# The order of sixteen products in a feed-forward block, and the place of one cast in the last gate

## The chip, the cores and the metric

The kernel runs on one core of a Trainium2 chip. The core has a matrix engine (TensorE, PE in the profile, with its weight loads listed apart as PEld), VectorE (DVE), ScalarE (ACT), GpSimd (POOL), and SyncE (SP), which issues most of the DMAs; GpSimd issues the rest. Each engine works its own instructions in the order in which they were written into its queue and waits on semaphores for the others. The metric is the device time of one execution in microseconds; the time before is the median of three runs.

## The reference

One layer of a streaming encoder on 512 frames of width 1024, all in float32:

```
h = h + 0.5 * swiglu(rmsnorm(h) , ffn1)          # 1024 -> 2 x 2816 -> 1024
z = rmsnorm(h) @ w_in                            # conv, attention and gate inputs
h = h + concat([conv_module(z), gated_linear_attention(z)]) @ w_out
h = h + 0.5 * swiglu(rmsnorm(h), ffn2)
gate = sigmoid(rmsnorm(h) @ ple_w_gate)          # 1024 x 1024
h = h + gate * (p @ ple_w_proj)                  # 256 -> 1024
out = rmsnorm(h)
```

where `swiglu(x) = (silu(gate) * up) @ w_out` and `gate, up` are the two halves of `x @ w_in`. The change touches the two `swiglu` blocks and the line with `gate`.

## The kernel before

**Numbers in two parts.** Every float32 operand of a product is split into a high part (a cast to fp32r on ScalarE, `high`, L216) and a low part (the operand minus its high part, on VectorE, `low`, L226; `parts`, L238, is both). A product is then three: high by high, high by low, low by high. Some low parts are made another way: ScalarE writes the negative and a DMA of GpSimd adds the operand onto it (`added`, L231). Weights lie in rings of six tiles, `wh` and `wl`.

**The feed-forward blocks** (`ffn`, L663) take two blocks of 128 columns of the hidden width at a time, a pair, and form the pair's gate and up values for all 512 frames by seven quarter products in place of eight (sums and differences of the weights' quarters, `Left`, L436, and of the activations' quarters, `Right`, L372). A quarter is 512 x 256 of weights by 512 x 256 of activations, so it has four blocks of rows (k) and two of columns (i). Five of the seven (`mul`, L341) are 24 products of 256 columns each. The other two, m7 (L744) and m4 (L752), go to both halves of the output, and are written as `mul2` (L357): the high weights times the activations' high and low parts side by side, one *wide* product of 512 columns, and the low weights times the high part, one *narrow* product of 256 columns. Both add into `pd`, a tile of two banks, one for each i. Ahead of m7 stands m6, which is narrow; ahead of m4 stands, in all pairs but one, a piece of the second product (`second`, L825), whose 512-column products read `act`. Of the first network nine pairs run this way, of the second ten. The order of TensorE, VectorE and ScalarE is here that of the program's text.

**The gate** (from L1770) is one more product by quarters, and in it the scheduler decides the order, bound only by what is needed and by the dependencies that the text adds: `act.behind(x, y)` puts x behind y on ScalarE (class `Ordered`, L36). Its names: `x_` and `w_` are two pairs of banks in which the quarters add up; `t1`, `t2`, `t3` are sums and differences of the weights' quarters. `t2` is made as a difference on VectorE, used, and then a DMA of GpSimd adds the last quarter of the weights onto it (L1803); the result, the second difference, has its parts in `b4` (L1821). `later_high` (L1773) is `high` with the cast put behind the instruction that `squared` names, the last of ScalarE when it was set, which is ahead of the gate.

`inputs(t, e)` (L1667) makes for a block of 128 frames and a half of the width the product with `p` (`pq`) and the transposed `h` (`pt`). `body` (L1714) takes the sum of the gate's product, forms the sigmoid on ScalarE, the product with `pq` and the sum with `pt` on VectorE (`cv`), then on ScalarE the squares of `cv` with their sum (the tile `u`), and multiplies `cv` by the final norm's gain `gfin` on VectorE. `kept` (L1761) copies a bank on ScalarE, `plus` (L1766) adds another bank to the copy on VectorE (tile `sq`).

The banks come from a ring of five with two spare (`bank`, L123). In the gate `x_` and `w_` hold four of the five, so `pq` and `pt` of `inputs(2, 1)`, which both come from the fifth, share it in turn: the transposes into `pt` can start when VectorE has read `pq`.

Of the kernel before, what the change touches and what calls it, by code (L numbers as in the profile page):

```python
# [15 lines left out]
P = 128  # L16
# [15 lines left out]
HALF = SEQ // 2  # L32
# [30 lines left out]
def block_kernel(ctx: ExitStack, tc: tile.TileContext, a: dict, out: bass.AP):  # L63
    nc = tc.nc
    pe, dve, act, pool = (Ordered(tc, e) for e in (nc.tensor, nc.vector, nc.scalar, nc.gpsimd))
# [38 lines left out]
    def tmp(s, w=SEQ, dt=F32, bufs=2):  # L104
        return tp.tile([P, w], dt, tag=s, bufs=bufs, name=nm(s))
# [17 lines left out]
    def bank():  # L123
        turn_no[0] += 1
        if not narrow_only[0] and turn_no[0] % 7 in (5, 6):
            return spare()
        return pp.tile([P, SEQ], F32, tag="mm", bufs=5, name=nm("ps"))
# [88 lines left out]
    def high(r3):  # L216

        nk, nc_ = r3.shape[1], r3.shape[2]
        hi = wp.tile([P, 1024], F32R, tag="wh", bufs=6, name=nm("wh"))
        lo = wp.tile([P, 1024], F32R, tag="wl", bufs=6, name=nm("wl"))  # L220
        h3 = hi[:, :nk * nc_].rearrange("p (k c) -> p k c", k=nk)
        l3 = lo[:, :nk * nc_].rearrange("p (k c) -> p k c", k=nk)
        act.copy(h3, r3)
        return h3, l3, r3

    def low(w, engine=dve):  # L226
        h3, l3, r3 = w
        engine.tensor_tensor(out=l3, in0=r3, in1=h3.bitcast(F32), op=ALU.subtract)
        return h3, l3
# [8 lines left out]
    def parts(r3):  # L238

        return low(high(r3))  # L240
# [20 lines left out]
    def rows_of(w, k):  # L261

        part, kk = (w[k // 4], k % 4) if isinstance(w, list) else (w, k)
        return part[0][:, kk, :], part[1][:, kk, :]
# [89 lines left out]
    def two(t):  # L354
        return t.rearrange("p (k c) -> p k c", k=2)

    def mul2(ps, w, x, first, last):  # L357

        wh, wl = w
        for k in range(4):  # L360
            both_, xh = x[k]
            for i in range(2):
                cs = slice(i * P, (i + 1) * P)
                pe.matmul(two(ps[:, i]), wh[:, k, cs], both_, start=(first and k == 0), stop=False, skip_group_check=True)
                pe.matmul(ps[:, i, 0:HALF], wl[:, k, cs], xh, start=False, stop=last and k == 3, skip_group_check=True)

    def sub(out, x, y):
        dve.tensor_tensor(out=out, in0=x, in1=y, op=ALU.subtract)
# [685 lines left out]
    ps = bank()  # L1054
    for k0 in range(0, DC, 4):
        for i in range(2):
            for j in range(4):
                pe.matmul(ps[2 * RANK * j:2 * RANK * (j + 1)], gw[:, k0 + j, :], hg[k0 + j][i].bitcast(F32),
                          start=(k0 == i == 0), stop=(k0 + i == 5), skip_group_check=True)
# [13 lines left out]
    for j in range(2):  # L1073
        ps = bank()
# [91 lines left out]
    def tokblock(w, t, mid={}):  # L1166

        ps = bank()
        ts = slice(t * P, (t + 1) * P)
        i = 0  # L1170
        for k in range(DC):
            wh, wl = w[k // 2][:2]
            xh, xl = hg[k]
            for x, y in ((xh, wh), (xl, wh), (xh, wl)):
                if i in mid:
                    mid[i]()
                pe.matmul(ps, x[:, ts], y[:, k % 2, :], start=(i == 0), stop=(i == 3 * DC - 1))
                i += 1
        return ps
# [31 lines left out]
    def chunk_sums(cs):  # L1211
        for j in range(2):
            if len(kvs) == j:
                kvs.append([bank(), bank()])
            for c in cs:
                s0 = (c % 2) * CH
                for i in range(2):
                    h = 2 * j + i
                    pe.matmul(kvs[j][c % 2][i * HK:(i + 1) * HK, (c // 2) * HV:(c // 2 + 1) * HV],
                              kdt[j][s0:s0 + CH, (c // 2) * P + i * HK:(c // 2) * P + (i + 1) * HK],  # L1220
                              vt[c // 2][s0:s0 + CH, h * HV:(h + 1) * HV], start=True, stop=True)
# [22 lines left out]
    def outputs(t2):  # L1244
        ops.extend([bank(), bank()])
        for t in (2 * t2, 2 * t2 + 1):
            for h in range(4):
                pe.matmul(out_of(t, h), sc[h][:, t, :], vt[t][:, h * HV:(h + 1) * HV],
                          start=(t % 2 == 0 and h < 2), stop=False, skip_group_check=True)
        for t in (2 * t2, 2 * t2 + 1):  # L1250
            for j in range(2):
                for i in range(2):
                    c = 2 * t + i
                    for h in (2 * j, 2 * j + 1) if c else ():
                        d = slice((h % 2) * HK, (h % 2 + 1) * HK)
                        pe.matmul(out_of(t, h)[i * CH:(i + 1) * CH], qdec[j][d, c * CH:(c + 1) * CH],
                                  states[j][c][0][d], start=False, stop=(t % 2 == j == 1), skip_group_check=True)
        for t in (2 * t2, 2 * t2 + 1):
            junk = tmp("sq", bufs=3)
            for h in range(4):  # L1260
                act.activation(junk[:, h * HV:(h + 1) * HV], out_of(t, h), AF.Square,
                               accum_out=so[:, 4 * t + h:4 * t + h + 1])
# [7 lines left out]
    for t in range(TB):  # L1270
        ps = tokblock(wv, t, {5: lambda: chunk_sums(range(6)),
                             8: lambda: wr.append(high(raw_r[2])),
                             14: lambda: wr.append(high(raw_r[3]))} if t == 3 else {})
# [57 lines left out]
    for t in range(TB):  # L1331
        if t == 0:
            taps(3)
            ps = tokblock(wr, t, {5: lambda: chunk_sums([6]), 12: lambda: outputs(0)})
            chain(range(4, 7))
            oload(4)
        elif t == 1:
            ps = tokblock(wr, t, {2: lambda: outputs(1)})
# [8 lines left out]
        else:  # L1347
            ps = tokblock(wr, t)
# [117 lines left out]
    for k in range(4):  # L1466
        for n in range(3):
            w, ps = half[n]
            wh, wl = rows_of(w, k)
# [70 lines left out]
    q11, q21, q12, q22, b11, b21, t2, wproj = ([] for _ in range(8))  # L1540
# [108 lines left out]
    def times(ps, x, w, first=False, last=False, blocks=((0, 1),), cols=slice(0, SEQ)):  # L1649

        for group in blocks:
            for k in range(4):
                xh, xl = x[k]
                wh, wl = (t[:, k % 2, cols] for t in w[k // 2][:2])
                for i in group:
                    ts = slice(i * P, (i + 1) * P)
                    o = ps[i][:, cols]
                    begin, end = first and k == 0, last and k == 3
                    pe.matmul(o, xh[:, ts], wh, start=begin, stop=False, skip_group_check=True)
                    pe.matmul(o, xl[:, ts], wh, start=False, stop=False, skip_group_check=True)  # L1660
                    pe.matmul(o, xh[:, ts], wl, start=False, stop=end, skip_group_check=True)
# [19 lines left out]
    def parts_of(t, e, z, pq, pt, c0=0, c1=SEQ, by=act):  # L1681

        cs = slice(c0, c1)
        first = t not in hf
        if first:
            hn = hf[t] = cvt()
        elif c0 == 0:
            hn = hl[t] = tmp("g1")
        else:
            hn = hl[t]  # L1690
        sg, junk = tmp("s"), tmp("u1")
        act.activation(sg[:, cs], z[:, cs], AF.Sigmoid, scale=rs[:, t:t + 1])
        yield
        dve.tensor_tensor(out=sg[:, cs], in0=sg[:, cs], in1=pq[:, cs], op=ALU.mult)
        yield
        dve.tensor_tensor(out=hn[:, cs], in0=pt[:, cs], in1=sg[:, cs], op=ALU.add)
        yield
        ss = ssf[:, 2 * t + 1 - first:2 * t + 2 - first] if c1 == SEQ else sse[:, 8:9]
        if by is dve:
            dve.scalar_tensor_tensor(out=junk[:, cs], in0=hn[:, cs], scalar=1.0, in1=hn[:, cs],  # L1700
                                     op0=ALU.mult, op1=ALU.mult, accum_out=ss)
        else:
            act.activation(junk[:, cs], hn[:, cs], AF.Square, accum_out=ss)

        base = sse[:, t:t + 1]
        if first:
            dve.tensor_tensor(out=hn, in0=hn, in1=gfin[e], op=ALU.mult)
            dve.tensor_scalar(base, ss, 1.0 / D, EPS, ALU.mult, ALU.add)
        elif c1 < SEQ:
            dve.scalar_tensor_tensor(out=base, in0=ss, scalar=1.0 / D, in1=base, op0=ALU.mult, op1=ALU.add)  # L1710

        yield

    def body(*args):  # L1714
        for _ in parts_of(*args):
            pass
# [44 lines left out]
    def kept(ps, name, **kw):  # L1761
        o = tmp(name, **kw)
        act.copy(o, ps)
        return o
# [6 lines left out]
    squared, summed = act.latest, dve.latest  # L1771

    def later_high(t):  # L1773

        w = high(t)
        act.behind(act.latest, squared)
        return w
# [27 lines left out]
    pool.on = False  # L1805
    body(0, 0, z0, *i0)
    body(1, 0, z1, *i1)
    b1 = [parts(t1[0])]
    both = tmp("m", 2 * SEQ, bufs=1).rearrange("p (f c) -> p f c", f=2)
    for i in range(2):  # L1810
# [7 lines left out]
    row_last(1)  # L1818
    project(1)
    times(x_, s1_, b1)  # L1820
    b4 = [parts(t) for t in t2]  # L1821
    x5 = [kept(p_, "sq", bufs=3) for p_ in x_]
    i2 = inputs(2, 1)
    z2 = plus(w_[0], x5[0])
# [66 lines left out]
```

## Time and profile before

| | us |
|---|---|
| runs shown | 944.18, 945.10, 945.73 |
| median | 945.1 |
| the profiled execution: its own time | 944.54 |
| its span, first to last instruction | 942.8 |
| TensorE busy | 929.8 (99%) |
| VectorE busy | 785.5 (83%) |
| ScalarE busy | 483.5 (51%) |
| the chain that ended last: TensorE's share | 96% |

A row of the page's groups reads: line, engine, operation, output and inputs by the program's names, shapes, count, then busy time and the mean of one in ns, then the engine's idle time ahead of it and who ended it. All operations are recorded by one helper, so each has the line L46, and tiles tell the places apart: `pd` is written by m7 and m4 alone, `t` is an operand of m7 and `hg` of m4. A row of the timeline reads: start and length in us, engine, line, operation, output and inputs, shapes, count, and in brackets the idle time ahead of it with its cause. Products on TensorE overlap, so the distance between two starts tells what one costs, not its length.

### The profile page before, as it was taken

Reading aid. Unit: us, or ns where it says so; the run is one execution under the profiler, and the core shown is the slowest. Engines: PE = TensorE matmul, PEld = TensorE weight load, DVE = VectorE, ACT = ScalarE, POOL = GpSimd, SP = SyncE. Lnnn points to the kernel's source line nnn. Section 1 sums busy time; section 2 is a strip of 40 time slices with the busy share of each in tenths; the row PEclk is TensorE's granted clock in tenths of the full one; section 3 lists DMA queues with packets and bytes.
Section 4 is the critical chain, followed back from the end, with each engine's and each line's share of the span. In section 5 each row is a group of like instructions: output and inputs, shape, how many; then the busy total and the mean of one; then the engine's idle time right before and its main releaser. Section 6 shows DMA issues by size and latency. Waiting matters only on the chain.

```text
span 942.8 us, 14171 instructions
## 1 busy us (share of the span) xinstructions
PE 929.8 (99%) x5611; PEld 816.0 (87%) x5611; DVE 785.5 (83%) x1077; ACT 483.5 (51%) x730; POOL 55.8 (6%) x74
## 2 busy tenths in 40 slices
PE   8999999999999999999999999999999999999996
PEld 7898999899989888788877889999899999988875
DVE  6798997898789676999986779988888878876986
ACT  5874444344444474463565875454334433446873
POOL 0100000000000111001120020000000000001120
PEclk9999999999999999999999999999999999999999
DMA  7633332342223593256552563432243224347463
GB/s 228 185 105 118 112 101 90 104 134 92 87 91 112 147 261 85 67 127 142 135 134 83 141 158 89 135 107 72 91 135 112 73 88 132 116 153 201 90 111 112
DMA packets 108134, 114.45 MB, mean 121 GB/s; under 512 B 5203, under 2 KB 96517, under 8 KB 108068
## 3 DMA queue, kind: packets, MB, share of 16 engines
q1 hardware_dynamic: 101748, 94.67, 32.7%
q0 software_dynamic: 6304, 18.88, 11.1%
q8 instruction: 44, 0.72, 0.3%
q14 instruction: 22, 0.18, 0.1%
q10 hardware_dynamic: 16, 0.00, 0.0%
HBM read 93.61 MB, written 2.10 MB: 102 GB/s over the span
## 4 chain that ended last, share of the span: by engine, by line
PE 96%; DMA 1%; DVE 1%; ACT 0%; SPq 0%; issue 0%; POOLq 0%; DVEq 0%; ACTq 0%
PE ps L46 84%; PE pd L46 11%; PE ax L46 1%; DMA sm<-in_ple_w_gate 1%; DMA wr<-in_ffn_w_in 1%; ACT wh L46 0%; SPq L538 0%; DVE s L46 0%; SPq L500 0%; DVE u L46 0%; DVE rs L46 0%; ACT yc L46 0%; DVE y L46 0%; DVE cv L46 0%; DVE g L46 0%
## 5 line engine op out<-in xcount | busy, mean ns | idle before, releaser
L46 PE MATMUL ps<-hg,wh 128*128 128x256 f32 (+1 forms) x1232 | 262.4, 312 | 1.2 <-ACT hg L46 1.2
L46 DVE TENSOR_TENSOR wl<-wr,wh 128x1024 fp32r<-128x1024 f32 (+2 forms) x161 | 188.1, 1179 | 38.2 <-ACT wh L46 38.1
L46 PEld LDWEIGHTS ps<-hg,wh 128*128 128x128 f32 x1232 | 201.3, 190 | 16.0 <-ACT hg L46 1.9
L46 ACT CAST wh<-wr 128x1024 fp32r<-128x1024 f32 (+2 forms) x178 | 177.7, 1020 | 49.3 <-DMA wr<-in_ffn_w_out 25.5
L46 PE MATMUL ps<-hg,wl 128*128 128x256 f32 (+1 forms) x616 | 187.6, 311 | 0.0
L46 PE MATMUL ps<-act,wh 128*128 128x512 f32 x512 | 157.9, 390 | 0.0
L46 ACT ACTIVATE s<-g 128x512 f32<-128x512 f32 x48 | 30.4, 632 | 192.2 <-DVE g L46 192.2
L46 PEld LDWEIGHTS ps<-hg,wl 128*128 128x128 f32 x616 | 117.0, 190 | 6.4
L46 PEld LDWEIGHTS ps<-act,wh 128*128 128x128 f32 x512 | 95.0, 188 | 19.0
L46 PE MATMUL ps<-t,wh 128*128 128x256 f32 x608 | 110.9, 283 | 0.0
L46 PE MATMUL ps<-act,wl 128*128 128x512 f32 x256 | 99.6, 389 | 0.0
L46 PEld LDWEIGHTS ps<-t,wh 128*128 128x128 f32 x608 | 95.7, 191 | 2.2
L46 PE MATMUL ps<-t,wl 128*128 128x256 f32 x304 | 86.0, 283 | 0.0
L46 DVE SCALAR_TENSOR_TENSOR cv<-glu,cw,cv 128x502 f32<-128x502 f32 (+24 forms) x90 | 61.8, 729 | 0.3
L46 DVE TENSOR_TENSOR wl<-sm,wh 128x1024 fp32r<-128x1024 f32 x42 | 51.2, 1221 | 8.8 <-ACT wh L46 8.8
L46 PEld LDWEIGHTS ps<-t,wl 128*128 128x128 f32 x304 | 58.2, 192 | 0.0
L46 PEld LDWEIGHTS ps<-act,wl 128*128 128x128 f32 x256 | 48.1, 188 | 10.1
L46 PE MATMUL ps<-wh,hg 128*128 128x512 f32 x176 | 54.7, 392 | 0.0
L46 PE MATMUL pd<-t,wh 128*128 128x512 f32 x152 | 54.6, 399 | 0.0
L46 PE MATMUL pd<-hg,wh 128*128 128x512 f32 x152 | 54.3, 397 | 0.0
L46 DVE SCALAR_TENSOR_TENSOR h<-ps,h 128x512 f32<-128x512 f32 x80 | 51.7, 683 | 2.5 <-PE ps L46 2.4
L46 ACT COPY sq<-ps 128x512 f32<-128x512 f32 x42 | 24.5, 586 | 56.9 <-PE ps L46 56.9
(307 smaller groups left out, 1568.4 us busy)
## 6 DMA issues: line engine op xcount, KB each, us to landing
wr<-in_ffn_w_in SPq DMA_DIRECT2D x84, 512.0 KB
wr<-in_ffn_w_out SPq DMA_DIRECT2D x32, 512.0 KB
wr<-in_w_in SPq DMA_DIRECT2D x20, 512.0 KB
wl<-wr POOLq DMA_DIRECT2D x18, 512.0 KB, 5.2
wr<-in_ffn_w_out SPq DMA_DIRECT2D x16, 384.0 KB
wr<-in_w_out SPq DMA_DIRECT2D x8, 512.0 KB
wq<-in_ple_w_gate SPq DMA_DIRECT2D x8, 512.0 KB
wl<-wq POOLq DMA_DIRECT2D x8, 512.0 KB, 4.9
```

The costliest lines, as they stand in the source:

```text
L46: inst = call(*args, **kwargs)
```

## The change

```diff
     def mul2(ps, w, x, first, last):
 
         wh, wl = w
-        for k in range(4):
-            both_, xh = x[k]
-            for i in range(2):
-                cs = slice(i * P, (i + 1) * P)
-                pe.matmul(two(ps[:, i]), wh[:, k, cs], both_, start=(first and k == 0), stop=False, skip_group_check=True)
-                pe.matmul(ps[:, i, 0:HALF], wl[:, k, cs], xh, start=False, stop=last and k == 3, skip_group_check=True)
+        at = [(k, i, slice(i * P, (i + 1) * P)) for k in range(4) for i in range(2)]
+        for k, i, cs in at:
+            pe.matmul(two(ps[:, i]), wh[:, k, cs], x[k][0], start=(first and k == 0), stop=False, skip_group_check=True)
+        for k, i, cs in at:
+            pe.matmul(ps[:, i, 0:HALF], wl[:, k, cs], x[k][1], start=False, stop=last and k == 3, skip_group_check=True)
...
     body(0, 0, z0, *i0)
     body(1, 0, z1, *i1)
+    squared = act.latest
     b1 = [parts(t1[0])]
...
     times(x_, s1_, b1)
-    b4 = [parts(t) for t in t2]
+    b4 = [low(later_high(t)) for t in t2]
     x5 = [kept(p_, "sq", bufs=3) for p_ in x_]
```

In `mul2` the eight wide products of a quarter product now follow each other, and the eight narrow ones follow them. In the gate the mark `squared` is set anew behind the second block's squares, and the two casts of the second difference go behind it. No instruction is added or taken away.

On TensorE, at the first m7, the order before (a row for each run of like instructions; the last figures are partitions and columns):

```order
L46 MATMUL ps_652<-t_109_565,wl_621 128x256
L46 MATMUL pd_797<-t_114_590,wh_648 128x512
L46 MATMUL pd_797<-t_114_590,wl_649 128x256
L46 MATMUL pd_797<-t_114_590,wh_648 128x512
L46 MATMUL pd_797<-t_114_590,wl_649 128x256
```

and now:

```order
L46 MATMUL ps_652<-t_109_565,wl_621 128x256
L46 MATMUL pd_797<-t_114_590,wh_648 128x512 x4
L46 MATMUL pd_797<-t_115_593,wh_648 128x512 x4
L46 MATMUL pd_797<-t_114_590,wl_649 128x256 x4
L46 MATMUL pd_797<-t_115_593,wl_649 128x256 x4
L46 MATMUL ps_652<-t_124_636,wh_644 128x256 x2
```

Wide and narrow took turns sixteen times in a block; now they change once. All 38 blocks change in this way.

On ScalarE, in the gate (`wh_8759` are the high parts of `p`'s weights, `wh_8789` and `wh_8793` those of the second difference, the `u` rows the squares of the first two blocks):

```order
 L46 CAST wh_8759<-pw_8329 128x512 x2
-L46 CAST wh_8789<-sm_8543 128x1024
 L46 ACTIVATE u_1380_8696,ssf_8513<-cv_8694 128x512
 L46 ACTIVATE u_1383_8705,ssf_8513<-cv_8703 128x512
+L46 CAST wh_8789<-sm_8543 128x1024
```

One cast went from ahead of the two squares to behind them. The scheduler moved one instruction of VectorE as well, at the same place (`wl_8751` is the low part of the first difference's second half, `s_8754` that of an activation):

```order
-L46 TENSOR_TENSOR wl_8751<-wq_8273,wh_8750 128x1024
 L46 TENSOR_TENSOR cv_8694<-cv_8694,gfin_8471 128x512
 L46 TENSOR_SCALAR sse_8514<-ssf_8513 128x1
 L46 TENSOR_TENSOR cv_8703<-cv_8703,gfin_8471 128x512
 L46 TENSOR_SCALAR sse_8514<-ssf_8513 128x1
+L46 TENSOR_TENSOR wl_8751<-wq_8273,wh_8750 128x1024
 L46 TENSOR_TENSOR s_8754<-s_1351_8547,s_8754 128x512
```

`wl_8751` went from ahead of the two multiplications by `gfin` to behind them. Further on, TensorE's order in the gate is the same before and now. There the second row's accumulation (`ps_8720`) and the transposes into `ps_8802`, the `pt` of `inputs(2, 1)`, wait for VectorE, and the rest of the accumulation stands behind the transposes:

```order
L46 MATMUL ps_8719<-wh_8789,hg_8421 128x512 [waits DVE_49]
L46 MATMUL ps_8719<-wh_8789,hg_8421 128x512
L46 MATMUL ps_8719<-wl_8790,hg_8421 128x512
L46 MATMUL ps_8720<-wh_8789,hg_8421 128x512 [waits DVE_49]
L46 MATMUL ps_8720<-wh_8789,hg_8421 128x512
L46 MATMUL ps_8802<-ident,h_100 128x128 [waits DVE_49]
```

The last wait is for VectorE's product that reads `ps_8801`, the `pq` of the same call.

## The prediction

> **What bounds the kernel now.** I read the page's span and its chain of waits first, then the two stages that the change touches: the quarter products in the two feed-forward networks by a table of windows and by TensorE's timeline, and the per-layer gate by the timelines of all engines.
>
> ```profile
> span 942.8 us, 14171 instructions
> PE 96%; DMA 1%; DVE 1%; ACT 0%; SPq 0%; issue 0%; POOLq 0%; DVEq 0%; ACTq 0%
> ...
> 60.00:330.00 270.00, 270.00 (x1741) 246.41 (x1741) 229.37 (x273) 113.53 (x150) 4.86 (x8) 1.00 0.36 107
> 566.00:850.00 284.00, 284.00 (x1858) 260.48 (x1857) 243.24 (x286) 120.05 (x156) 0.00 (x0) 1.00 0.35 108
> ```
>
> TensorE sets the time: it is 96% of the chain, and the two windows, which cover nearly all of both networks, show it busy 270.00 of 270.00 and 284.00 of 284.00 us at a granted clock of 1.00. VectorE is busy 229 of 270 and 243 of 284 us there, so 15% of its time is spare. A nanosecond saved between two products therefore shortens the span, and a wait removed on another engine doesn't.
>
> **The quarter products.** `mul2` runs twice for each pair (m7, m4): 8 wide products (high weights, 512 columns) and 8 narrow ones (low weights, 256 columns). No product, load or cast is added or removed; only the order on TensorE changes.
>
> ```profile
> 65.63 2.83 PE pd L46 x16
> 79.68 2.81 PE pd L46 x16
> ...
> L46 PE MATMUL pd<-t,wh 128*128 128x512 f32 x152 | 54.6, 399 | 0.0
> L46 PE MATMUL pd<-hg,wh 128*128 128x512 f32 x152 | 54.3, 397 | 0.0
> ```
>
> The first two rows are of the chain (start, length, count), the others of the groups by line and shape. 304 wide products are 38 blocks of 8, 19 of m7 and 19 of m4. A block takes 2.83 us where narrow products stand ahead of it (m7) and 2.81 where wide ones do (m4, but for one), alternating. The durations of about 398 ns overlap, so I use the distance from start to start. What the new order costs can be read off where the kernel already runs wide behind wide and narrow behind narrow:
>
> ```profile
> 74.05 0.40 PE L46 MATMUL ps<-actH,wh 128*128 128x512 f32 x1
> 74.29 0.40 PE L46 MATMUL ps<-actL,wh 128*128 128x512 f32 x1
> ...
> 75.44 0.61 PE L46 MATMUL ps<-act,wh 128*128 128x512 f32 x2
> 75.89 0.39 PE L46 MATMUL ps<-act,wl 128*128 128x512 f32 x1
> ...
> 79.52 0.39 PE L46 MATMUL pd<-hg,wh 128*128 128x512 f32 x1
> 79.75 0.28 PE L46 MATMUL pd<-hg,wl 128*128 128x256 f32 x1
> ```
>
> ```profile
> 122.00 0.40 PE L46 MATMUL ps<-t,wh 128*128 128x256 f32 x2
> ...
> 122.95 0.28 PE L46 MATMUL ps<-t,wl 128*128 128x256 f32 x1
> ```
>
> At 74.05 a run of wide products starts behind narrow ones: 8 of them reach to 75.89, 1.84 us, the first at 0.24, later ones at 0.227 (18 from 75.44 to 79.52, 4.08 us). At 122.00 narrow products start behind wide ones: 8 of them reach to 122.95, 0.95 us. So an m7 block becomes 1.84 + 0.95 = 2.79 (was 2.83), an m4 block 8 x 0.227 + 0.95 = 2.77 (was 2.81): about 0.043 us each, 38 x 0.043 = 1.6 us. Put differently, a wide product costs about 0.01 us more behind a narrow one, today eight times in a block, then once. Bounds: if the last wide product, with a narrow one behind it, keeps its dearer step, 0.009 us a block is lost and 1.3 remain; if the dear first steps vanish too, a block is 8 x 0.227 + 8 x 0.119 = 2.77 in both cases and 1.8 is gained. I take 1.6.
>
> A wide product reads its activations in two pieces of 256 columns and changes the bank with each product. The first wide product of the m4 block, at 79.52 behind other wide ones, has both habits and its successor starts 0.23 later, so I charge nothing for them. The second half of the activations is wanted about 0.5 us earlier than now; were it just in time today, one such block would lose up to 0.5, but the two windows show no wait at all, so I charge nothing. The narrow products want the low weights 1.6 us later than today, a slack that no wait asks for.
>
> **The gate.** Here is the one stall of TensorE's tail.
>
> ```profile
> 907.21 0.39 PE L46 MATMUL ps<-wh,s 128*128 128x512 f32 x1
> 909.81 0.50 PE L46 MATMUL ps<-wh,s 128*128 128x512 f32 x1 [2.22 <-DVE s L46]
> 910.15 0.40 PE L46 MATMUL ps<-wl,s 128*128 128x512 f32 x1
> ...
> 916.80 0.60 PE L46 MATMUL ps<-ident,h 128*128 128x128 f32 x4
> ```
>
> ```profile
> 902.52 0.63 ACT L46 CAST wh<-pw 128x512 fp32r<-128x512 f32 x1
> 906.04 1.05 ACT L46 CAST wh<-sm 128x1024 fp32r<-128x1024 f32 x1 [2.89 <-DMA sm<-in_ple_w_gate]
> 906.99 0.62 ACT L46 ACTIVATE u<-cv 128x512 f32<-128x512 f32 x1
> 907.62 0.61 ACT L46 ACTIVATE u<-cv 128x512 f32<-128x512 f32 x1
> 908.57 1.04 ACT L46 CAST wh<-sm 128x1024 fp32r<-128x1024 f32 x1 [0.24 <-DMA sm<-in_ple_w_gate]
> ...
> 911.99 0.59 ACT L46 COPY sq<-ps 128x512 f32<-128x512 f32 x1 [0.38 <-PE ps L46]
> 913.45 0.57 ACT L46 COPY sq<-ps 128x512 f32<-128x512 f32 x1
> 914.89 1.32 ACT L46 ACTIVATE s<-sq,rs 128x512 f32<-128x512 f32 x2
> ```
>
> ```profile
> 902.83 0.68 DVE L46 TENSOR_TENSOR cv<-ax,s 128x512 f32<-128x512 f32 x1
> 903.82 1.22 DVE L46 TENSOR_TENSOR wl<-wq,wh 128x1024 fp32r<-128x1024 f32 x1
> 907.74 0.69 DVE L46 TENSOR_TENSOR cv<-cv,gfin 128x512 f32<-128x512 f32 x1 [2.70 <-ACT u L46]
> 909.08 0.68 DVE L46 TENSOR_TENSOR s<-s,s 128x512 fp32r<-128x512 f32 x1
> ...
> 913.95 1.28 DVE L46 TENSOR_TENSOR sq<-ps,sq 128x512 f32<-128x512 f32 x2
> ...
> 915.74 1.27 DVE L46 TENSOR_TENSOR s<-s,ps 128x512 f32<-128x512 f32 x2
> ...
> 920.34 0.14 DVE L46 TENSOR_SCALAR sse<-ssf 128x1 f32<-128x1 f32 x1
> 921.12 1.37 DVE L46 TENSOR_TENSOR m<-ps,m 128x512 f32<-128x512 f32 x2 [0.64 <-PE ps L46]
> ```
>
> Read upward from 909.81: TensorE waits for a low part (DVE s, 909.08), which stands behind two multiplications by `gfin` (from 907.74), which wait for ScalarE's squares (906.99), which stand behind the cast of the second difference, which waits for its DMA until 906.04. The change puts the squares ahead of that cast. The cast itself loses nothing by it: the squares are done before its DMA lands, and so the casts queued behind it stand where they stood; GpSimd's and SyncE's queues keep their order. In the times of the old trace: the casts of `pw` end at 903.15, VectorE's second `cv` at 903.51, so the squares run to about 904.3; the two multiplications with their small ops (1.34 from 907.74 to 909.08) run 903.8 to 905.2, the moved `wl` (1.22) to 906.4, the low part to 907.0. TensorE wants it at 907.44 (907.21 + 0.23) and `wl` later still, so that stall goes, with 0.4 us to spare.
>
> Now what is late next. TensorE would run on 2.4 us earlier, but ScalarE doesn't: both casts still wait for DMAs that land at about 906.0 and 908.5, and from 908.57 it works without a pause to 911.61, where it waited 0.38 for the product that it copies. That 0.38 is all that it gains: copies at 911.61 and 913.07, sigmoid at 914.51. VectorE's second sum follows the second copy, 913.7 to 914.35. TensorE ran without a pause from 909.81 to the transposes at 916.80, with two products of the second row just ahead of them (from 916.34); from 907.44 it would reach that row at about 913.9 and waits there for 0.5. Behind it stand the four transposes (916.80 in the trace): in the order they wait for VectorE's product that frees the bank, and that follows the sigmoid, 915.36 to 916.04 where it was 915.74 to 916.42. The transposes start at 916.08 in place of 916.80: 0.72 earlier. Less the dearer first product after a wait (909.81 to 910.15 is 0.34 in place of 0.23), 0.6 us remains of a stall of 2.4. Bounds: 0.4, ScalarE's own gain, and 2.4, if the two later waits were no waits. VectorE's small work between (to 920.48 in the trace, 0.38 earlier then) ends at 920.1, before the next sums at 921.12 - 0.6 = 920.5 need it, so the rest of the tail moves with TensorE.
>
> **Sum.** 1.6 + 0.6 = 2.2 us. The profiled execution took 944.5 us (span 942.8, 1.7 around it) and becomes 942.3; it lies 0.6 below the median shown, 945.1. Against that median the forecast is 942.9 us.
>
> **The rivals.** *The blocks don't care about order*, and only the gate gains: 945.1 - 0.6 = 944.5. For it: the same sixteen products stream the same columns. Against it: 0.227 and 0.119 in pure runs add to less than the 0.352 of today's pairs. [...] Chance 0.12.
>
> *The whole stall is won*: the waits at 914.4 and 916.1 don't form because the DMAs land earlier. 945.1 - 1.6 - 2.4 = 941.1. Against it: what issues those DMAs is untouched. Chance 0.08.
>
> *The wide products are slow in this place themselves*, by their two-piece operand or the change of bank, not by their neighbour:
>
> ```profile
> 80.21 0.40 PE L46 MATMUL pd<-hg,wh 128*128 128x512 f32 x1
> ...
> 80.45 0.28 PE L46 MATMUL pd<-hg,wl 128*128 128x256 f32 x1
> ```
>
> Inside a block they do take 0.24. Then a block is 8 x 0.24 + 0.95 = 2.87, 0.05 over today's 2.82: 1.9 us lost, 945.1 + 1.9 - 0.6 = 946.4, slower than before. It turns slower from a wide step of (2.82 + 0.016 - 0.95) / 8 = 0.236 on. Against it: the 0.23 at 79.52. Chance 0.12; a step over 0.242 would carry it past 947.0.
>
> **How the numbers follow.** The forecast has 0.68, its own range 942.6 (1.8 + 0.7, nothing lost at the restart) to 943.4 (1.3 + 0.4). With the indifferent order inside, the range is 941.3 to 944.7, which leaves out the fully won stall and the slow wide products, 0.20. A measurement of this kernel tells about 0.2% from no change, that is 943.2 and 947.0. Faster: 0.61 of the forecast's 0.68 and the 0.08 of the won stall, 0.69. Same: the rest of the forecast, 0.07, the 0.12 of the indifferent order and half of the slow wide products, 0.25. Slower: 0.06.
>
> **What would show it.** In the chain, blocks of 16 at 2.79 and 2.77 us in place of 2.83 and 2.81; wide steps of 0.227 from the fifth on. In the gate, the squares at once behind the casts of `pw`, no wait for the low part near 907, and two new waits on TensorE about 7 us later in sum nearly as long as the old one. Blocks at 2.82 or more, or wide steps of 0.236, would make the first term wrong; a second sum or a sigmoid that comes more than 0.4 us earlier against the DMA's landing, the second.

## The result and the profile after

The changed kernel takes 941.66 us (median of 7 runs, 941.34 to 942.36), the kernel before 944.32 us (median of 7, 944.18 to 945.94): a ratio of 0.9968, 95% interval 0.9956 to 0.9979, so 0.32% faster. The forecast was 942.9 us, in a range of 941.3 to 944.7. It was set against a median of three runs, 945.1, which these seven put at 944.3. The medians lie 2.66 us apart where 2.2 were forecast; the interval of the ratio reaches from 2.0 to 4.2 us, so the times alone don't tell the two apart, and the terms are judged by the traces.

| | before | after |
|---|---|---|
| median, us | 944.32 | 941.66 |
| profiled execution, us | 944.54 | 941.44 |
| its span, us | 942.8 | 939.7 |
| all 38 blocks of quarter products, us | 107.22 | 105.65 |
| TensorE's waits in the gate, us | one of 2.2 | two, 0.3 and 0.8 |

The blocks' sum is the distance from the first product of a block to the first one behind it, added over the 38 blocks of the trace. Of the two waits, 0.8 is the profile's idle time, as 2.2 is; 0.3 is read from the starts (911.58 to 912.10, 0.52 in place of 0.23), of which the profile counts 0.12 as idle.

The chain of waits of the changed kernel (start, length, count), first blocks of the first network and the stretch after the gate's stall:

```profile
PE 97%; DMA 1%; ACT 1%; DVE 1%; issue 0%; POOLq 0%; ACTq 0%; DVEq 0%
...
65.13 2.79 PE pd L46 x16
79.15 2.77 PE pd L46 x16
93.14 2.79 PE pd L46 x16
110.41 2.77 PE pd L46 x16
124.40 2.79 PE pd L46 x16
...
913.66 8.19 PE ps L46 x39
```

TensorE is still the chain. The same blocks read 2.83 and 2.81 before, and the alternation of m7 and m4 is kept. That TensorE still has no pause in the second network is in the table of windows (length, then busy time of TensorE, its weight loads, VectorE, ScalarE, GpSimd, then granted clock):

```profile
566.00:850.00 284.00, 284.00 (x1856) 261.00 (x1855) 243.59 (x286) 119.40 (x156) 0.00 (x0) 1.00 0.35 107
```

Earlier wanted activations and later wanted low weights made no wait. Inside a block, on TensorE's timeline (start, time from the first start to the last modelled end):

```profile
64.97 2.00 PE L46 MATMUL pd<-t,wh 128*128 128x512 f32 x8
66.81 1.12 PE L46 MATMUL pd<-t,wl 128*128 128x256 f32 x8
67.76 0.40 PE L46 MATMUL ps<-t,wh 128*128 128x256 f32 x2
...
78.99 1.98 PE L46 MATMUL pd<-hg,wh 128*128 128x512 f32 x8
80.80 1.11 PE L46 MATMUL pd<-hg,wl 128*128 128x256 f32 x8
81.76 0.40 PE L46 MATMUL ps<-hg,wh 128*128 128x256 f32 x2
```

Starts are what counts: the m7 block's wide part reaches from 64.97 to 66.81, 1.84, its narrow part to 67.76, 0.95; the m4 block's 1.81 and 0.96. These are the two numbers that the forecast had taken from other places of the kernel.

The gate, on TensorE, ScalarE and VectorE (in square brackets the idle time ahead and what ended it):

```profile
911.58 0.39 PE L46 MATMUL ps<-wl,hg 128*128 128x512 f32 x1
912.10 0.73 PE L46 MATMUL ps<-wh,hg 128*128 128x512 f32 x2
913.66 0.66 PE L46 MATMUL ps<-ident,h 128*128 128x128 f32 x4 [0.83 <-DVE s L46]
914.07 0.47 PE L46 MATMUL ps<-wl,hg 128*128 128x512 f32 x1
914.39 0.62 PE L46 MATMUL ps<-wh,hg 128*128 128x512 f32 x2
```

```profile
900.02 1.15 ACT L46 CAST wh<-pw 128x512 fp32r<-128x512 f32 x2
901.06 0.64 ACT L46 ACTIVATE u<-cv 128x512 f32<-128x512 f32 x1
...
901.68 0.62 ACT L46 ACTIVATE u<-cv 128x512 f32<-128x512 f32 x1
...
903.85 1.05 ACT L46 CAST wh<-sm 128x1024 fp32r<-128x1024 f32 x1 [1.45 <-DMA sm<-in_ple_w_gate]
906.37 1.06 ACT L46 CAST wh<-sm 128x1024 fp32r<-128x1024 f32 x1 [1.46 <-DMA sm<-in_ple_w_gate]
...
908.80 0.61 ACT L46 CAST s<-s 128x512 fp32r<-128x512 f32 x1
909.32 0.57 ACT L46 COPY sq<-ps 128x512 f32<-128x512 f32 x1
...
912.18 1.32 ACT L46 ACTIVATE s<-sq,rs 128x512 f32<-128x512 f32 x2
```

```profile
904.30 0.68 DVE L46 TENSOR_TENSOR s<-s,s 128x512 fp32r<-128x512 f32 x1
...
911.35 0.69 DVE L46 TENSOR_TENSOR sq<-ps,sq 128x512 f32<-128x512 f32 x1 [0.74 <-ACT sq L46]
...
912.92 1.30 DVE L46 TENSOR_TENSOR s<-s,ps 128x512 f32<-128x512 f32 x2 [0.28 <-ACT s L46]
```

The squares follow the casts of `pw` at once (901.06), the low part is done at 904.98, and TensorE runs past the place of the old stall. It stops twice later, as forecast: at the second row of the accumulation, which starts at 912.10 behind VectorE's second sum (911.35 + 0.69), and at the transposes (913.66), behind VectorE's product that frees their bank (912.92 and half of 1.30). Both of those wait for ScalarE.

Where the profile's 3.10 us went: 0.50 to the first microseconds, which the change doesn't touch, 1.40 to the two networks, 1.12 to the gate and 0.08 to the rest. The blocks' own sum fell by 1.57, but the networks are only 1.40 shorter. From the first product of a network's first block to the tenth behind its last block, the first network takes 259.54 us before and 258.87 after, the second 279.56 and 278.83. So 0.17 is given back behind the blocks: in each pair of the first network one step among the `act` products is 7 to 8 ns longer than before. The gate's 1.12 is what TensorE gains from the casts of `pw` on (902.00 before, 900.02 after, 1.98) to the end. In the first microseconds the kernel before waited for `hg`, and the changed one in this execution didn't:

```profile
7.82 1.17 PE L46 MATMUL ps<-hg,wh 128*128 128x512 f32 x4
9.89 1.19 PE L46 MATMUL ps<-hg,wh 128*128 128x512 f32 x4 [0.90 <-ACT hg L46]
```

```profile
8.17 2.30 PE L46 MATMUL ps<-hg,wh 128*128 128x512 f32 x8
```

The first rows are of before, the last of after. Of seven experiments whose kernels all start alike, one shows that wait (0.70) and six don't, so it is scatter between executions and no gain. The change's own 1.40 + 1.12 = 2.52 lies near the 2.66 of the medians and inside the interval.

### The profile page after: what moved, and what is told of

Its sections match the earlier page's. It is cut to its first block, busy times and chain, and to the rows that moved or that the text cites. A ratio compares the mean times of both kernels' runs of the same rounds, so it can differ in the third digit from the quotient of the medians.

```text
span 939.7 us, 14172 instructions
## 1 busy us (share of the span) xinstructions
PE 929.2 (99%) x5611; PEld 816.8 (87%) x5611; DVE 785.9 (84%) x1077; ACT 483.1 (51%) x730; POOL 55.9 (6%) x74
## 4 chain that ended last, share of the span: by engine, by line
PE 97%; DMA 1%; ACT 1%; DVE 1%; issue 0%; POOLq 0%; ACTq 0%; DVEq 0%
PE ps L46 84%; PE pd L46 11%; PE ax L46 1%; DMA sm<-in_ple_w_gate 1%; ACT s L46 0%; DVE s L46 0%; ACT wh L46 0%; ACT wl L46 0%; ACT sq L46 0%; DVE u L46 0%; DVE rs L46 0%; ACT yc L46 0%; DVE y L46 0%; DVE g L46 0%; DVE lnsq L46 0%
## 5 line engine op out<-in xcount | busy, mean ns | idle before, releaser
L46 ACT CAST wh<-sm 128x1024 fp32r<-128x1024 f32 x42 | 43.8, 1043 | 5.3 <-DMA sm<-in_ple_w_gate 2.9
L46 DVE TENSOR_TENSOR u<-pd,u 128x512 f32<-128x512 f32 x57 | 39.3, 689 | 5.9 <-PE pd L46 4.6
```

Of the source, the lines that this page charges most:

```text
L46: inst = call(*args, **kwargs)
```

## Experiments

The theory after the result: the blocks gain 1.6 us because a wide product costs more behind a narrow one, and the gate gains about 1.1 us, where the forecast had 0.6, limited by ScalarE. Rivals: that the gate's surplus belongs to the blocks or to scatter, and that something other than the change of width makes the blocks dear.

**The blocks alone.** The kernel before with only `mul2` changed:

```diff
-        for k in range(4):
-            both_, xh = x[k]
-            for i in range(2):
...
+        at = [(k, i, slice(i * P, (i + 1) * P)) for k in range(4) for i in range(2)]
+        for k, i, cs in at:
+            pe.matmul(two(ps[:, i]), wh[:, k, cs], x[k][0], start=(first and k == 0), stop=False, skip_group_check=True)
+        for k, i, cs in at:
+            pe.matmul(ps[:, i, 0:HALF], wl[:, k, cs], x[k][1], start=False, stop=last and k == 3, skip_group_check=True)
```

> The kernel before with the new order of the sixteen products alone. My theory: the two edits add up, and the blocks carry 1.6 us of the 2.7 by which the medians of before (944.3) and changed kernel (941.7) differ: blocks of 2.79 and 2.77 us, the wait of 2.2 us for DVE s in the gate as before, 942.7. Rival: the blocks' gain is partly given back at the gate's stall, which is fixed by a DMA: then the stall grows and the time is 943.5 or more.

Measured: 942.42 us (median of 11), the kernel before 944.97 (median of 21), ratio 0.9981 [0.9972, 0.9990], a gain of 1.8 us [0.9, 2.6]. The medians lie 2.55 apart; three of the eleven runs took 943.9 to 944.6, the others 942.3 to 942.8. The blocks add up to 105.65 us and the networks are 1.40 us shorter, both as in the changed kernel. In TensorE's timeline the gate's stall is there in full:

```profile
905.10 0.39 PE L46 MATMUL ps<-wh,s 128*128 128x512 f32 x1
907.57 0.50 PE L46 MATMUL ps<-wh,s 128*128 128x512 f32 x1 [2.08 <-DVE s L46]
```

So the block term is right in mechanism and, by the trace, in size, and takes nothing from the gate.

**The gate alone.** The kernel before with only the moved casts:

```diff
     body(1, 0, z1, *i1)
+    squared = act.latest
     b1 = [parts(t1[0])]
...
-    b4 = [parts(t) for t in t2]
+    b4 = [low(later_high(t)) for t in t2]
```

> The kernel before with the moved mark and casts alone. My theory: 1.1 us, 943.2, blocks of 2.83 and 2.81, the wait for DVE s gone and two short waits later, where the second sum and the transposes are. Rival: my forecast of 0.6 was right and the rest of the profiled difference was chance in when the DMAs landed: 943.7.

Measured: 943.37 us (median of 11), ratio to the same runs of before 0.9984 [0.9975, 0.9993], a gain of 1.5 us [0.7, 2.4]. The blocks are as before, 107.22 us. In the trace TensorE waits in the gate as in the changed kernel:

```profile
913.06 0.74 PE L46 MATMUL ps<-wh,hg 128*128 128x512 f32 x2
914.63 0.66 PE L46 MATMUL ps<-ident,h 128*128 128x128 f32 x4 [0.83 <-DVE s L46]
```

Against the casts of `pw`, which stand 0.98 earlier than before here (901.02 for 902.00), the transposes come 2.17 earlier (914.63 for 916.80): 1.2 us from the gate. So the surplus lies in the gate and not in the blocks. Whether it is the change's or chance, this run alone doesn't tell: 1.5 [0.7, 2.4] covers 0.6 and 1.1, and the DMA landed early in this trace too. The second cast of `sm`, which waits for it, starts 6.31 us behind the first cast of `pw`, where it is 6.35 in the changed kernel and 6.57 before. The traces below in which it landed as before settle it. The two parts add up within their intervals: 0.19% and 0.16%, 0.32% together in the changed kernel.

**Is ScalarE the limit in the gate?** In the changed kernel, the four casts for the gate's last product (two of weights, two of activations) go behind the second sigmoid on ScalarE:

```diff
         act.copy(hi, src[jp])
+        if sigmoid[0] is not None and src is n2 and b22_turn:
+            act.behind(act.latest, squared)
         sub(lo, src[jp], hi.bitcast(F32))
...
+    sigmoid, b22_turn = [None], []
...
         act.activation(sg[:, cs], z[:, cs], AF.Sigmoid, scale=rs[:, t:t + 1])
+        sigmoid[0] = act.latest
...
-    b22 = [added(high(t)) for t in q22]
+    squared = sigmoid[0]
+    b22_turn.append(1)
+    b22 = [added(later_high(t)) for t in q22]
```

> The changed kernel, with the four casts for the gate's last product (weights and activations) put behind the second sigmoid of the next two blocks on ScalarE. My theory: what is left of the stall is ScalarE's queue, where these casts stand ahead of the two copies and the two sigmoids for which TensorE waits: both short waits go, the transposes start about 1.4 us earlier, and the time falls by 1.3 us to 940.4. Rival: the second difference's DMA, VectorE or a bank sets the transposes' start: at most 0.3 us are gained, 941.4, or the late casts hold up the last product and it is slower.

Measured: 940.26 us (median of 5), ratio to before 0.9956 [0.9944, 0.9969]. By the trace the scheduler moved a little more than the four casts: the two low parts of the activations on VectorE follow them, one negative low part of the weights on ScalarE (`ACTIVATE wl<-wq`) now stands ahead of the sigmoids, and one product of TensorE went behind the transposes. ScalarE and TensorE in its trace:

```profile
906.98 1.05 ACT L46 CAST wh<-sm 128x1024 fp32r<-128x1024 f32 x1 [1.46 <-DMA sm<-in_ple_w_gate]
908.15 1.32 ACT L46 COPY sq<-ps 128x512 f32<-128x512 f32 x2
...
911.28 1.32 ACT L46 ACTIVATE s<-sq,rs 128x512 f32<-128x512 f32 x2
912.50 1.98 ACT L46 CAST wh<-wq 128x1024 fp32r<-128x1024 f32 x2
```

```profile
912.49 0.40 PE L46 MATMUL ps<-wh,hg 128*128 128x512 f32 x1
912.76 0.66 PE L46 MATMUL ps<-ident,h 128*128 128x128 f32 x4
913.17 0.47 PE L46 MATMUL ps<-wh,hg 128*128 128x512 f32 x1
```

Measured from its DMA's landing the first copy comes 1.2 us behind the start of the cast of `sm` (908.15 - 906.98), 2.95 in the changed kernel (909.32 - 906.37), and TensorE has no wait left in the gate; of all its waits (total, count, longest) three are in the first 11 us and the last, for `yc`, is at 508 us:

```profile
PE ps L46 <- DVE zeros L46: 1.1, 1, 1.1
PE ps L46 <- ACT hg L46: 0.9, 2, 0.7
PE ps L46 <- ACT yc L46: 0.2, 1, 0.2
```

Against the casts of `pw` (900.74 here, 902.00 before) the gate gains 2.5 us: the whole stall. It is the fastest version here, 1.4 us below the changed kernel by the medians, and shows that the limit left by the change was ScalarE's queue and not the DMA alone. The size is from one trace, in which the second cast of `sm` starts 6.25 us behind the first of `pw`, 0.32 sooner than before; had the DMA landed as before, up to 0.3 of the 2.5 would be missing, by an estimate from these starts.

**What makes a block dear?** Four other orders of the same sixteen products, one run each. Groups of two (two wide, two narrow, and so on):

```diff
-        for k, i, cs in at:
-            pe.matmul(two(ps[:, i]), wh[:, k, cs], x[k][0], start=(first and k == 0), stop=False, skip_group_check=True)
-        for k, i, cs in at:
...
+        for j in range(0, 8, 2):
+            for k, i, cs in at[j:j + 2]:
...
+            for k, i, cs in at[j:j + 2]:
...
```

> The changed kernel with the sixteen products in groups: two wide, two narrow, four times over. Theory one: a wide product behind narrow ones costs more by a transient that ebbs over about five products (233, 236, 227, 234, 230, then 227 ns in the changed kernel), a narrow one behind wide ones less (114, 118, then 120): a block of m7 is 4 x (233 + 236 + 114 + 118) = 2.804 us. Theory two: each change of width costs the same; from eight changes at 2.832 and one at 2.793, 0.0056 us each, four make 2.810. The difference to the run in groups of four tells them apart: none by theory one, 0.011 us by theory two.

Measured: 941.47 us, blocks 105.72 us, m7 2.787 and m4 2.777. Neither theory's number held: the m7 block is shorter than with groups of eight (2.793). That called for two more theories. In the kernel before, each narrow product adds to the half of the accumulator that the wide one ahead of it has just added to; groups of two end that. So I let widths take turns again, but on different halves (of the fifteen steps inside a block two stay on one half, the one to the tenth product and the last):

```diff
-        at = [(k, i, slice(i * P, (i + 1) * P)) for k in range(4) for i in range(2)]
...
+        order = [(0, 0, 1), (0, 0, 0), (1, 0, 1), (0, 1, 0), (1, 1, 1), (0, 2, 0), (1, 2, 1), (0, 3, 0), (1, 3, 1),
+                 (0, 1, 1), (1, 0, 0), (0, 2, 1), (1, 1, 0), (0, 3, 1), (1, 2, 0), (1, 3, 0)]
+        for narrow, k, i in order:
...
```

> The changed kernel, but in each quarter product wide and narrow products take turns again (wide to narrow seven times in a block, eight before the change), in an order in which, but for the last two, no product adds to the same half of the accumulator as the one ahead of it. In the kernel before, each narrow product adds to the half that the wide one ahead of it has just added to. Theory A, the change of width is dear by itself (39 and 44 ns a block for seven returns from narrow to wide inside it; here six): m7 blocks 2.83, m4 2.80, all 38 together 107.0 us, about 942.8 us. Theory B, a narrow product right behind a wide one on the same half is dear, for which the groups of two (105.72 us) speak: blocks as after the change, 2.79 and 2.77, together 105.7 us, about 941.5.

Measured: 942.76 us (before, beside it: 943.88), blocks 106.87 us. In the chain, first two rows of the run with groups of two, for comparison, then the same two of this run:

```profile
65.09 2.79 PE pd L46 x16
79.10 2.78 PE pd L46 x16
```

```profile
65.31 2.82 PE pd L46 x16
79.35 2.81 PE pd L46 x16
```

The accumulator's half isn't the main cause: turns are dear on different halves too. The converse, eight wide and eight narrow, but one half after the other:

```diff
-        at = [(k, i, slice(i * P, (i + 1) * P)) for k in range(4) for i in range(2)]
+        at = [(k, i, slice(i * P, (i + 1) * P)) for i in range(2) for k in range(4)]
```

> The changed kernel, but the eight wide products go four to the first half of the accumulator and then four to the second, the eight narrow ones likewise: six of seven steps in a run stay on one half, none did so in a run before. Theory A (the change of width is dear): as after the change, 2.79 and 2.77, 105.65 us together, 941.5 us. Theory B in its wide form (any product behind another on the same half is dear, by up to the 39 to 44 ns over eight such steps of the kernel before, about 5 ns each): twelve such steps a block, 60 ns, 107.9 us together, 943.8 us.

Measured: 941.47 us, blocks 105.65 us, 2.793 and 2.766 as in the changed kernel, to the nanosecond. Products behind each other on one half cost nothing extra. And groups of four, the edit of the groups of two with 4 in place of 2:

> The changed kernel with groups: four wide, four narrow, four wide, four narrow products. Theory A (each return from narrow to wide costs the 39 to 44 ns over seven, about 6 ns): one return inside a block, m7 2.80, m4 2.77, together 105.9 us, 941.8 us. Theory B (a narrow one behind a wide one on the same half): none of those, 2.79 and 2.77, 105.7 us, 941.5 us. The two lie close; the steps at the return (0.233 or 0.227) tell more than the time.

Measured: 941.93 us, blocks 106.17 us, m7 2.807 and m4 2.780. It lies above groups of two and of eight, and above what either theory said. Theory one of the groups of two had asked for the same m7 block in both, theory two for groups of four to be 0.011 us shorter; they are 0.020 longer. All orders, with the price of a block beyond 8 x 227 + 8 x 120 = 2776 ns (steps deep inside a run of one width), and by how much both networks together are shorter than before:

| order | m7 block, ns | m4 block, ns | beyond 2776, ns | 38 blocks, us | networks shorter by, us |
|---|---|---|---|---|---|
| turns, same half (before) | 2832 | 2810 | 56, 34 | 107.22 | 0 |
| turns, other half | 2818 | 2806 | 42, 30 | 106.87 | 0.30 |
| groups of four | 2807 | 2780 | 31, 4 | 106.17 | 1.01 |
| groups of two | 2787 | 2777 | 11, 1 | 105.72 | 1.53 |
| groups of eight (the change) | 2793 | 2766 | 17, -10 | 105.65 | 1.40 |

The steps from start to start, read from the single records of an m7 block, say how: in the kernel before, with turns, a wide one takes 233 to 241 ns and a narrow one 113 to 120; in the run of eight behind narrow ones the wide steps are 234, 235, 229, 232, 231 and then 227, so the surcharge lasts for five products and not for one; and a narrow one just behind wide ones takes 113 or 119 and gives some of it back. With groups of two the steps repeat 233, 236, 116, 112, 233, 231, 113, 119: the narrow ones give back nearly all. So the change of width is dear and the half isn't, but the price isn't so much for each change: six changes back to wide in the turns on different halves cost 25 ns over groups of eight in an m7 block, and three in groups of two cost nothing. Over the whole networks groups of two are even 0.13 us ahead of groups of eight, since they give nothing back behind the blocks; a difference that small doesn't show in the times (941.47 in one run, 941.66 as a median). A wide product here also has another weight tile and another operand than a narrow one, but the start of a block shows that the width ahead counts and not these: behind wide products of other tiles (m4) its first step is 227 ns, behind narrow ones of other tiles (m7) 233. The one m4 block with narrow products ahead takes 2794 ns in the changed kernel, as the m7 blocks do. What in TensorE makes the steps so stays open.

## Why the forecast came out as it did

**TensorE bounds the kernel**: right. The blocks are 41 ns shorter on average, the networks 37 ns for each block, and no other engine took over (the window above, 284.00 of 284.00).

**The blocks, 1.6 us**: right. 107.22 - 105.65 = 1.57, forecast 2.79 and 2.77, measured 2.793 and 2.766. Its picture, that a wide product is dearer once in a block, was too simple: the surcharge lasts for five products, and the row of a run elsewhere in the kernel (1.84 for eight) contained that, which is why the sum held. That the picture was too simple and the size still came out is in part luck: 0.17 of the 1.57 is given back behind the blocks, of which the forecast knew nothing, and 1.40 still lies within its bounds of 1.3 to 1.8. (The upper bound is 1.9 by its own figures, 19 x 0.06 + 19 x 0.04.) Nothing charged for the two-piece operand, the bank, the activations wanted earlier or the low weights wanted later: right, the pure steps are 227 ns in the block as elsewhere.

**The gate, 0.6 us**: here is the step that failed, by its size: 1.1 us in the trace, of which 0.9 are the change's own. What was wrong is the sentence "That 0.38 is all that it gains" and what is added up from it. The forecast's own sign against this term was a sigmoid more than 0.4 us earlier against the DMA's landing; it came 0.51 earlier. The mechanism was as forecast: the old stall gone, two new waits where they were looked for, TensorE behind ScalarE and VectorE. But the two are not nearly as long as the old one: from start to start the old stall cost 2.5 us (2.37 ahead of 909.81 and 0.11 behind it), and the new waits cost 1.4 (0.29 and 1.10). In the time of the trace before (1.98 added, by which the casts of `pw` stand earlier after):

| | before | forecast | measured |
|---|---|---|---|
| squares done | 908.2 | 904.3 | 904.28 |
| low part done | 909.8 | 907.0 | 906.96 |
| second cast of `sm` starts | 908.57 | 908.5 | 908.35 |
| first copy | 911.99 | 911.61 | 911.30 |
| sigmoid | 914.89 | 914.51 | 914.16 |
| product that frees the bank | 915.74 | 915.36 | 914.90 |
| transposes | 916.80 | 916.08 | 915.64 |
| second `wh,hg` row behind them | 917.47 | 916.87 | 916.37 |

The way into the gate came out to 0.05 us; the 0.5 that the forecast missed lies behind it, in four pieces that all had one sign:

- ScalarE was to gain 0.38, its idle time: it gained 0.51 from the second cast on (0.13 more). I counted to the end of the operation ahead (911.61), but without a wait ScalarE starts an operation about 0.1 before the one ahead ends: 908.80 + 0.61 is 909.41, and the copy starts at 909.32.
- "915.36 to 916.04" for VectorE's product moves it by ScalarE's gain alone. Before, VectorE itself was late: the low parts of `sm` (911.67, 2.35 long) held the sums up to 913.95, and from there it worked without a pause to the product at 915.74. Now it idles ahead of each sum and 0.28 ahead of the product, and gains 0.11 more.
- The DMA landed 0.22 earlier against the casts of `pw` than before. That isn't the gate's edit: with the blocks alone, the casts of `pw` come 2.09 earlier (899.91) and the first cast of `sm` 2.25 (903.79), and TensorE gains 0.20 there without the gate's edit. It is scatter: from its issue on GpSimd to its landing, the second of these two DMAs took 9.46 us before, 9.26 in the changed kernel, and 9.17 to 9.47 in the seven experiments.
- The restart, "less the dearer first product after a wait", 0.1, cost 0.05.

0.13 + 0.11 + 0.22 + 0.05 is 0.51, and 0.6 + 0.5 = 1.1. Without the landing, the change's own share is 0.9 us, inside the bounds of 0.4 to 2.4 that the forecast had set and above the 0.6 it took. Three of the orders above bear this out, for they have the gate's edit and a DMA that landed about as before. ScalarE and TensorE with one half first:

```profile
899.85 1.15 ACT L46 CAST wh<-pw 128x512 fp32r<-128x512 f32 x2
906.38 1.06 ACT L46 CAST wh<-sm 128x1024 fp32r<-128x1024 f32 x1 [1.46 <-DMA sm<-in_ple_w_gate]
```

```profile
913.68 0.66 PE L46 MATMUL ps<-ident,h 128*128 128x128 f32 x4 [0.83 <-DVE s L46]
914.10 0.47 PE L46 MATMUL ps<-wl,hg 128*128 128x512 f32 x1
914.41 0.62 PE L46 MATMUL ps<-wh,hg 128*128 128x512 f32 x2
```

The second cast stands 6.53 behind the first of `pw` (6.57 before), and the last row comes 3.06 earlier than its 917.47 before, the casts of `pw` 2.15: 0.91 from the gate. Groups of two and of four give 0.90 and 0.91 so measured, and the three traces in which that cast comes 0.22 to 0.26 earlier (the changed kernel, the gate alone, the turns on different halves) 1.11 to 1.14. That these pieces sit on ScalarE's path is shown by the casts behind the sigmoid, where the path is shortened and both waits go; the split of the rest is read from one trace of each kernel.

**The rivals.** The indifferent order (944.5) fell with the blocks alone: 1.40 us over the networks in the trace. The Trainium skill ("TensorE: Matmul & The Clock Gate", "Back-to-back issue gap") gives for a warm matmul by itself a gap of its columns over 2.4 GHz plus 2.5 ns, and says that in a stream of weight loads and matmuls both set the spacing. The formula has no term for the order, so sixteen products would take an estimated 8 x (215.8 + 109.2) = 2600 ns in any; here they took 2832 or 2793 ns. The fully won stall (941.1) didn't come, for the reason given, ScalarE's queue; it came when its casts were moved. The slow wide products (946.4) fell: their steps are 227 ns.

**The level.** The forecast is taken from the median of three runs, 945.1. The seven runs beside the changed kernel put that median at 944.3 and the 21 beside the experiments at 945.0, while the means of both are 944.8. So the base moves by up to 0.7 us from series to series, and how much of the 1.24 us between 942.9 and 941.66 is the base and how much the gain can't be told from the times. In the trace, without the first microseconds, the gain is 2.6 us for 2.2.

## What to carry to other kernels

When a stall is removed, write the chain that is late next operation by operation from starts, not from ends, and ask of each engine on it whether it was waiting or was itself late: an engine that was late can gain more than the one it follows (0.11 us here). Then look at what stands in that engine's queue and isn't wanted yet: four casts moved behind a sigmoid brought as much again as the change at that place (1.4 us). Of products of two widths, don't let them take single turns, and measure the order over the whole stretch, since the price doesn't follow the number of changes and part of it falls behind the block; and take the base of a forecast from many runs when the gain is 0.3%.

## What was unexpected

- Groups of two (105.72 us for 38 blocks) are as good as groups of eight (105.65) and over the whole networks 0.13 us better, and groups of four (106.17) worse than both; single turns cost 107.22.
- A product's step depends on its width and on up to five products ahead of it: 227 ns for 512 columns and 120 for 256 in a run, 224 to 241 for a wide one after narrow ones, 112 to 120 for a narrow one after wide ones.
- Two products behind each other on one half of the accumulator cost the same as on two halves (2793 and 2766 ns in both).
